# One common offset modulo 512 bytes for all tensor-engine tiles, later scaling and splitting of the key latents, and four gate-weight buffers in an attention layer

## The chip, the core and the metric

The kernel runs on one core of a Trainium2 chip. The metric is device time in microseconds (us): the median of three runs before is 604.2 us (603.97 to 605.96). TensorE is PE in the profile, with PEld for its weight loads; VectorE is DVE, ScalarE is ACT, GpSimd is POOL, SyncE is SP. SP only issues DMAs here.

## The reference

One layer of multi-head latent attention over x (1024 tokens by 1024 channels, fp32), then a final norm. Eight heads; a query/key width of 128 plain and 64 rotary columns; 384 query latents and 256 key/value latents.

```
h = rms_norm(x, g)
proj = h @ w_in                       # c_q 384, c_kv 256, k_pe 64, gate 1024
q = rms_norm(c_q, q_norm) @ w_uq      # per head: 128 plain, 64 rotary
kv = rms_norm(c_kv, kv_norm) @ w_ukv  # per head: 128 key, 128 value
q_pe, k_pe = apply_rope(q_pe), apply_rope(k_pe)
s = q_nope . k_nope + q_pe . k_pe     # times 192 ** -0.5
o = softmax(s) @ v
out = rms_norm(x + (o * silu(gate)) @ w_out, final_norm)
```

## The kernel before

Every product is made in three matmuls. An operand is held as a high and a low part in fp32r (`wh`, `wl`; `xh`, `xl`), and `mm3` (L58 to L61) adds high x high, high x low and low x high into PSUM. Such a pair comes from `split` (L63): POOL writes the high part (L64), DVE subtracts it and writes the low part (L65).

The stages, in program order:

1. L157 to L187: the query latents. Eight steps over the input channels, each with 18 matmuls of 512 columns; xh and xl of the step are made on the way.
2. `rstd_x` (L208) computes the row norms of x; `stream(3)` and `stream(4)` (L245) the key latents `craw[3]`, `craw[4]` with 48 matmuls each. `stream` loads its weights in two halves `gwr` (256 KB each), splits them into `gwh` and `gwl` and multiplies; `gwh` and `gwl` have two buffers each (the pool `gp`, L115), `gwr` has two.
3. `latent_norm` (L233) makes a row of 1/rms for the query latents ("rq") and for the key latents ("rk"). The row goes to DRAM (`rq_d`, `rk_d`) and comes back broadcast to all partitions in `gate[:, 7]`; then DVE scales the latents with it (L243). The scaled query latents are split into cq_h, cq_l (L311, L312), the scaled key latents into kv_h (POOL, L315) and kv_l (DVE, L316).
4. `stream_gate(0)` to `stream_gate(7)` (L261): the output gate, tiles g_6 to g_13, 48 matmuls each. Between them stand four `rope_half` (L340), two head groups g by two halves of the tokens: 18 matmuls into two PSUM tiles `ab`, the rotation on DVE and POOL (L353 to L355), a high copy on ACT (L356), a low part on DVE (L357), and four DMA writes of 256 KB to `qpe_d` in DRAM (L359). t0, t1, hi and lo live in three `rooms` (L338), taken in turn. The weights of a head group are two `load_q` (L366): a load into `wq_r`, which has one buffer (tag `w_r`, shared with the wk and wv loads), and a split.
5. Attention (L434 to L499): 64 score tiles s, each two halves of five matmuls with 512 columns (`q` with `k`, then `qpe` with `kk`), softmax, exchange through DMA, and values: 32 tiles pv of 24 matmuls with 256 columns. k, q and v of a head are made between them.
6. The output projection (L501 to L619): eight token tiles for the first half of the output columns, eight for the second, eight heads of three matmuls each. Its weights `woh`, `wol` of the first half have a pool of their own (but the last head's); those of the second half lie in the places of v, q and, for heads 6 and 7, of `kk_h`, `kk_l` (L519).

A tile scheduler sets the order of the instructions on each engine when the program is built; DMAs of one engine are issued in order. The pools set the addresses in SBUF. In the built program the scratch for DMAs takes the first 16384 bytes of each partition, and the pools follow. The offset of a tile within its partition, modulo 512 bytes, comes out like this (before): xh, xl, gwh, gwl, wpe 288; wh, wl of the first stage 256; cq_h, cq_l, kv and the weights wq, wk 256; q, k, v, qpe, wv and o_split 480; kk 192; pt 352; woh, wol 256 in the first output half, and 480 or 192 (the places of kk) in the second.

Of the kernel before, what the change touches and what calls it, by code (L numbers as in the profile page):

```python
# [8 lines left out]
F32 = mybir.dt.float32  # L9
F32R = mybir.dt.float32r  # L10
AF = mybir.ActivationFunctionType
ALU = mybir.AluOpType
AX = mybir.AxisListType

P = 128
# [5 lines left out]
QR = 384  # L21
KR = 256
EPS = 1e-6
KD = D // P
# [5 lines left out]
def kernel(  # L30
# [21 lines left out]
    nc = tc.nc  # L52
    mm = nc.tensor.matmul

    def f32(ap):
        return ap.bitcast(F32)
# [24 lines left out]
    const = ctx.enter_context(tc.tile_pool(name="const", bufs=1))  # L81
# [3 lines left out]
    ps_t = pctx.enter_context(tc.tile_pool(name="ps_t", bufs=2, space=bass.MemoryType.PSUM))  # L85
    ps_a = pctx.enter_context(tc.tile_pool(name="ps_a", bufs=2, space=bass.MemoryType.PSUM))

    g_sb = const.tile([P, KD + 5], F32, name="g_sb")
    qpe_d = dram.tile([H, 4, 32, L], F32, name="qpe_d")

    row_d = {name: dram.tile([P, KD], F32, name=f"{name}_d") for name in ("rx", "sq", "sk", "rq", "rk")}
    kk_h = const.tile([P, L], F32R, name="kk_h")
    kk_l = const.tile([P, L], F32R, name="kk_l")

    def acc(name):
        return ps_a.tile([P, 512], F32, name=name, tag="acc")
# [4 lines left out]
    def halves(half):  # L101
        return slice(half * HT, (half + 1) * HT)
# [3 lines left out]
    def turned_tile(name):  # L106
        return turned.tile([P, 4, L], F32, name=name, tag="g")

    home = [turned_tile("craw_a"), turned_tile("craw_b")]
    craw = [home[0][:, i] for i in range(4)] + [home[1][:, 0]]  # L110


    xctx = ExitStack()
    xs = xctx.enter_context(tc.tile_pool(name="xs", bufs=1, side="right"))
    gp = xctx.enter_context(tc.tile_pool(name="gp", bufs=2, side="right"))  # L115
    xp = xctx.enter_context(tc.tile_pool(name="xp", bufs=1, side="right"))
    xh = xp.tile([P, KD, L], F32R, name="xh")
    xl = xp.tile([P, KD, L], F32R, name="xl")
# [15 lines left out]
    def rsqrt(v, s, r):  # L134

        nc.scalar.activation(s, v, AF.Sqrt)
        nc.vector.reciprocal(r, s)
        nc.vector.scalar_tensor_tensor(s, r, -0.5, r, op0=ALU.mult, op1=ALU.mult)
        nc.vector.tensor_mul(s, s, v)
        nc.vector.scalar_tensor_tensor(r, s, 1.5, r, op0=ALU.add, op1=ALU.mult)  # L140

    with ExitStack() as wctx:
# [14 lines left out]
        for k in range(KD):  # L157
# [13 lines left out]
            for hs in [halves(0), halves(1)] if k == 0 else [slice(0, L)]:  # L171
# [3 lines left out]
                    op0=ALU.mult, op1=ALU.subtract,  # L175
# [4 lines left out]
            for m, half in units:  # L180
                ms, hs = slice(m * P, (m + 1) * P), halves(half)
# [8 lines left out]
    gate = gpool.tile([P, H, L], F32, name="gate")  # L190
# [3 lines left out]
    kv_h = kvp.tile([P, 2, L], F32R, name="kv_h")  # L194
    kv_l = kvp.tile([P, 2, L], F32R, name="kv_l")
    rx_sb = xs.tile([P, L], F32, name="rx_sb")
    small = xs.tile([P, 6, KD], F32, name="small")
    ssx, mx, rx, v_s, s_s, r_s = (small[:, i] for i in range(6))

    def row_of(name):  # L200
        return row_d[name].rearrange("p j -> (p j)").unsqueeze(0)

    def spread(name, compact, row):

        nc.sync.dma_start(row_d[name], compact)
        nc.sync.dma_start(row, row_of(name).partition_broadcast(P))
# [23 lines left out]
            nc.scalar.copy(line[:, halves(half)], total(cs, half, name)[0:1])  # L230
        nc.sync.dma_start(row_of(name), line)

    def latent_norm(ms, sums, n, name, row):  # L233

        nc.sync.dma_start(v_s, row_d[sums])
        nc.vector.tensor_mul(v_s, v_s, mx)
        nc.vector.tensor_scalar(v_s, v_s, 1.0 / n, EPS, op0=ALU.mult, op1=ALU.add)
        rsqrt(v_s, s_s, r_s)
        nc.vector.tensor_mul(r_s, r_s, rx)
        spread(name, r_s, row)  # L240
        for m in ms:
            c = craw[m]
            nc.vector.scalar_tensor_tensor(c, c, g_sb[:, KD + m:KD + m + 1], row, op0=ALU.mult, op1=ALU.mult)  # L243
# [17 lines left out]
    def stream_gate(i):  # L261
        ps = stream(6 + i)
        gt = gate[:, i]
        nc.vector.tensor_mul(gt, ps, rx_sb)
        nc.scalar.activation(gt, gt, AF.Silu)
# [4 lines left out]
    latent_sums((0, 1, 2), "sq")  # L270
    ps = stream(4)
    nc.scalar.copy(craw[4], ps)
    latent_norm((0, 1, 2), "sq", QR, "rq", gate[:, 7])
    latent_sums((3, 4), "sk")


# [26 lines left out]
        nc.scalar.copy(kk_h[d], kp[0:DR])  # L303
        nc.vector.tensor_sub(kk_l[d], kp[0:DR], f32(kk_h[0:DR]))

    latent_norm((3, 4), "sk", KR, "rk", gate[:, 7])
    cqp = cctx.enter_context(tc.tile_pool(name="cqp", bufs=1))
    cq_h = [cqp.tile([P, L], F32R, name=f"cq_h{m}") for m in range(3)]
    cq_l = [cqp.tile([P, L], F32R, name=f"cq_l{m}") for m in range(3)]
# [1 line left out]
        nc.scalar.copy(cq_h[m], craw[m])  # L311
        nc.vector.tensor_sub(cq_l[m], craw[m], f32(cq_h[m]))  # L312
    stream_gate(0)
    for m in range(2):
        nc.gpsimd.tensor_scalar(kv_h[:, m], craw[3 + m], 1.0, 1.0, op0=ALU.mult, op1=ALU.mult)  # L315
        nc.vector.tensor_sub(kv_l[:, m], craw[3 + m], f32(kv_h[:, m]))  # L316

    def load_split(shape, src, tag, bufs, pool=None):
        pool = pool or wts
        wh = pool.tile(shape, F32R, name=f"{tag}_h", tag=f"{tag}_h", bufs=bufs)  # L320
# [6 lines left out]
    def load_q(src):  # L327
        return load_split([P, 3, P], src, "wq", 2)
# [6 lines left out]

    rope_sb = home[1][:, 1:3]
    nc.sync.dma_start(rope_sb, rope_q.rearrange("c p t -> p c t"))
    rooms = [(home[0][:, 0], home[0][:, 1]), (home[0][:, 2], home[0][:, 3]), (home[1][:, 0], home[1][:, 3])]  # L338

    def rope_half(g, half, w):  # L340

# [18 lines left out]

    for i in range(1, H):
        stream_gate(i)
        if i < 5:
            g, half = (i - 1) // 2, (i - 1) % 2
            if half == 0:
                w_rope = [load_q(wqp[2 * g + j]) for j in range(2)]  # L366
            rope_half(g, half, w_rope)
# [4 lines left out]


    ps_a = ctx.enter_context(tc.tile_pool(name="ps_b", bufs=4, space=bass.MemoryType.PSUM))
    at = ctx.enter_context(tc.tile_pool(name="attn", bufs=2, side="right"))

    def split_tiles(name):
        hi = at.tile([P, 2, HT], F32R, name=f"{name}_h", tag="pt_h", bufs=3)
# [57 lines left out]
    def scores(u, q, kx, qpe):  # L436
        half, qs = (u % 8) // 4, slice((u % 4) * P, (u % 4 + 1) * P)
        s = wide("s")
        qpe_s = qpe[half][:, qs]
        for kb in range(2):  # L440
            ks = halves(kb)
            mm3(s[:, ks], q[half][0][:, qs], q[half][1][:, qs], kx[kb][0], kx[kb][1], True, False)
            mm(s[:, ks], lhsT=qpe_s, rhs=kk_h[:, ks], start=False, stop=False)  # L443
            mm(s[:, ks], lhsT=qpe_s, rhs=kk_l[:, ks], start=False, stop=True)  # L444
        if u % 4 == 0:
            square[u // 4] = turned_tile("probs").rearrange("p j (k t c) -> p j k t c", k=8, t=4)
        p_t = square[u // 4][:, :, :, u % 4]
        nmx = at.tile([P, 1], F32, name="nmx", tag="nmx", bufs=4)
        nc.vector.tensor_reduce(nmx, s, axis=AX.X, op=ALU.max, negate=True)  # L449
        sm = at.tile([P, 1], F32, name="sm", tag="sm", bufs=4)  # L450
        nc.scalar.activation(  # L451
            p_t.rearrange("p j k c -> p k j c"), s.rearrange("p (k j c) -> p k j c", k=8, j=4),
            AF.Exp, bias=nmx, accum_out=sm,
        )
        rc = at.tile([P, 1], F32, name="rc", tag="rc", bufs=4)
        nc.vector.reciprocal(rc, sm)  # L456
        nc.gpsimd.tensor_scalar(p_t, p_t, rc, 1.0, op0=ALU.mult, op1=ALU.mult)  # L457
        nc.vector.transpose(out=p_t, in_=p_t)  # L458
# [63 lines left out]
        (nc.vector if k % 2 else nc.gpsimd).tensor_sub(wl, wr, f32(wh))  # L522
        w_o[nh].append((wh, wl))

    ss = const.tile([P, 2, KD], F32, name="ss")

    def out_start(nh, t, product=True):

        ts = slice(t * P, (t + 1) * P)
# [58 lines left out]

    def out_rstd(t):
        mean_square(t, 1)  # L590
        s, r = (at.tile([P, 1], F32, name=f"y{c}", tag=f"y{c}") for c in "sr")
        rsqrt(ss[:, 0, t:t + 1], s, r)
        return r

# [28 lines left out]
    for u in range(U + 10):  # L623
        h, i = u // 8, u % 8
# [129 lines left out]
```

## Time and profile before

| what | value |
|---|---|
| runs, median of 3 | 604.2 us |
| profiled execution | 605.06 us |
| its span (first to last instruction) | 603.0 us |
| PE busy | 585.5 us, 97% |
| DVE / ACT / POOL busy | 71% / 46% / 36% |

The profiled execution is 0.86 us above the median, and 2.06 us of it lie outside the span. A matmul's busy time in the profile (0.39 us) overlaps the next one's, so the pace of PE is read from the distance between the starts of two matmuls. In rows of the timeline the last bracket gives the idle time ahead of the instruction and what ended it.

### The profile page before, as it was taken

How to read it: one execution, taken by the hardware profiler on the slowest of the kernel's cores; microseconds unless marked ns; L12 is line 12 of the kernel's file. 1: busy time of each engine (PE TensorE's matmuls, PEld its weight loads, DVE VectorE, ACT ScalarE, POOL GpSimd, SP SyncE). 2: the span in 40 equal slices, each digit the busy share in tenths (PEclk: the TensorE clock that was granted, in tenths of full speed). 3: DMA queues.
4: the chain of work that ended last, by engine and by line, in shares of the span. 5: the costliest groups of instructions: out<-in, count | busy, mean ns of one | idle time of the engine just before them, and what ended most of it. 6: DMA issues, size and time to landing. Idle time of an engine off the chain costs nothing.

```text
span 603.0 us, 8667 instructions
## 1 busy us (share of the span) xinstructions
PE 585.5 (97%) x2988; PEld 492.5 (82%) x2988; DVE 429.6 (71%) x632; ACT 277.3 (46%) x435; POOL 218.7 (36%) x195
## 2 busy tenths in 40 slices
PE   9999999898999999999999999999999979999995
PEld 6888878676778888888988889888888868978885
DVE  5613587537414789899878899798987996783663
ACT  4348562102102564556554545454545573653642
POOL 3314502324211344554334354334542663563000
PEclk9999999989999999999999999999999999999999
DMA  8646322242411175566654747356645975431332
GB/s 311 237 119 238 96 72 56 74 129 80 156 48 58 39 170 125 123 149 143 153 128 109 177 107 160 91 128 154 138 101 131 262 180 142 116 103 52 123 139 104
DMA packets 35534, 78.71 MB, mean 131 GB/s; under 512 B 7266, under 2 KB 10850, under 8 KB 35428
## 3 DMA queue, kind: packets, MB, share of 16 engines
q1 hardware_dynamic: 34196, 76.08, 47.0%
q10 hardware_dynamic: 1296, 2.10, 0.9%
q8 instruction: 23, 0.38, 0.3%
q14 instruction: 19, 0.16, 0.1%
HBM read 36.19 MB, written 8.41 MB: 74 GB/s over the span
## 4 chain that ended last, share of the span: by engine, by line
PE 65%; DVE 10%; DMA 10%; issue 6%; SPq 4%; ACT 3%; POOL 2%; ACTq 0%; DVEq 0%; POOLq 0%
PE o L59 4%; PE o L60 4%; PE o L61 4%; PE pv L59 4%; PE pv L60 4%; PE pv L61 4%; PE s L443 4%; PE s L444 4%; PE s L59 4%; PE s L60 4%; PE s L61 4%; SPq L468 3%; PE g L61 3%; PE g L59 3%; PE g L60 3%
## 5 line engine op out<-in xcount | busy, mean ns | idle before, releaser
L457 POOL TENSOR_SCALAR probs<-probs,rc 128x1024 f32<-128x1024 f32 x64 | 82.1, 1285 | 109.5 <-DVE rc L456 88.6
L451 ACT ACTIVATE probs<-s,nmx 128x1024 f32<-128x1024 f32 x64 | 71.4, 1115 | 71.2 <-DVE nmx L449 67.3
L476 ACT CAST pt_h<-d 128x1024 fp32r<-128x1024 f32 x64 | 66.0, 1051 | 45.6 <-PE pv L61 20.1
L458 DVE STREAM_TRANSPOSE probs<-probs 128x1024 f32<-128x1024 f32 x64 | 78.8, 1233 | 6.4 <-POOL probs L457 5.8
L449 DVE TENSOR_REDUCE nmx<-s 128x1 f32<-128x1024 f32 x64 | 76.9, 1207 | 6.8 <-PE s L444 6.6
L59 PE MATMUL pv<-pt_h,v_h 128*128 128x256 f32 x256 | 72.3, 283 | 2.0 <-ACT pt_h L476 2.0
L60 PE MATMUL pv<-pt_l,v_h 128*128 128x256 f32 x256 | 72.1, 282 | 0.9 <-DVE pt_l L478 0.9
L61 PE MATMUL pv<-pt_h,v_l 128*128 128x256 f32 x256 | 71.9, 281 | 0.0
L61 PE MATMUL g<-xh,gwl 128*128 128x512 f32 x160 | 64.2, 401 | 4.6 <-DVE gwl L65 4.6
L59 PE MATMUL g<-xh,gwh 128*128 128x512 f32 x160 | 63.8, 399 | 0.9 <-POOL gwh L64 0.8
L481 POOL TENSOR_TENSOR pt_l<-d,pt_h 128x512 fp32r<-128x512 f32 x32 | 47.9, 1496 | 45.1 <-ACT pt_h L476 25.9
L60 PE MATMUL g<-xl,gwh 128*128 128x512 f32 x160 | 63.3, 396 | 0.0
L59 PEld LDWEIGHTS pv<-pt_h,v_h 128*128 128x128 f32 x256 | 48.2, 188 | 4.4 <-ACT pt_h L476 3.0
L59 PE MATMUL s<-k_h,q_h 128*128 128x512 f32 x128 | 50.4, 396 | 1.2 <-ACT probs L451 1.2
L60 PEld LDWEIGHTS pv<-pt_l,v_h 128*128 128x128 f32 x256 | 48.1, 188 | 3.5 <-DVE pt_l L478 1.1
L443 PE MATMUL s<-kk_h,qpe 128*128 128x512 f32 x128 | 50.7, 396 | 0.0
L444 PE MATMUL s<-kk_l,qpe 128*128 128x512 f32 x128 | 50.7, 396 | 0.0
L60 PE MATMUL s<-k_l,q_h 128*128 128x512 f32 x128 | 50.3, 393 | 0.0
L61 PE MATMUL s<-k_h,q_l 128*128 128x512 f32 x128 | 50.2, 392 | 0.0
L61 PEld LDWEIGHTS pv<-pt_h,v_l 128*128 128x128 f32 x256 | 48.2, 188 | 2.4
L478 DVE TENSOR_TENSOR pt_l<-d,pt_h 128x1024 fp32r<-128x1024 f32 x32 | 42.8, 1337 | 6.5 <-ACT pt_h L476 4.8
L60 PE MATMUL o<-wol,o_split 128*128 128x512 f32 (+1 forms) x118 | 45.1, 382 | 0.0
(194 smaller groups left out, 1288.5 us busy)
## 6 DMA issues: line engine op xcount, KB each, us to landing
d<-probs SPq DMA_DIRECT2D x256, 128.0 KB, 2.4
gwr<-in_wg SPq DMA_DIRECT2D x20, 256.0 KB, 3.0
craw_b<-in_x SPq DMA_DIRECT2D x8, 512.0 KB, 6.6
qpe<-qpe_d SPq DMA_DIRECT2D x16, 256.0 KB, 3.1
wor<-in_wo SPq DMA_DIRECT2D x16, 256.0 KB, 3.2
xr<-in_x SPq DMA_DIRECT2D x16, 256.0 KB, 2.6
xr<-in_xT SPq DMA_DIRECT2D x7, 512.0 KB, 6.5
qpe_d<-craw_a SPq DMA_DIRECT2D x12, 256.0 KB
```

The source lines that it names most:

```text
L59: mm(ps, lhsT=lh, rhs=rh, start=first, stop=False)
L60: mm(ps, lhsT=lh, rhs=rl, start=False, stop=False)
L61: mm(ps, lhsT=ll, rhs=rh, start=False, stop=last)
L443: mm(s[:, ks], lhsT=qpe_s, rhs=kk_h[:, ks], start=False, stop=False)
L444: mm(s[:, ks], lhsT=qpe_s, rhs=kk_l[:, ks], start=False, stop=True)
L449: nc.vector.tensor_reduce(nmx, s, axis=AX.X, op=ALU.max, negate=True)
L451: nc.scalar.activation(p_t.rearrange("p j k c -> p k j c"), s.rearrange("p (k j c) -> p k j c", k=8, j=4), AF.Exp, bias=nmx, accum_out=sm,)
L457: nc.gpsimd.tensor_scalar(p_t, p_t, rc, 1.0, op0=ALU.mult, op1=ALU.mult)
L458: nc.vector.transpose(out=p_t, in_=p_t)
L476: nc.scalar.copy(hi, src)
L478: nc.vector.tensor_sub(lo, src, f32(hi))
L481: nc.gpsimd.tensor_sub(lo[:, 1], src[:, 1], f32(hi[:, 1]))
```

## The change

- The DMA scratch is 1024 bytes in place of 16384, two unused tiles (`pad_a`, `pad_b`) are put into the pool `const`, `ss` moves there, `small` is longer, and the one-column tiles of the softmax and of the last norm move into a pool `columns`. In the built program every tile that a matmul reads then lies at offset 480 modulo 512 bytes.
- `gwh`, `gwl` get four buffers each in place of two.
- `latent_norm` only makes the row; the scaling is a function `latent_scale`. That of the query latents is called after the rotary key is made (L312 after), that of the key latents after stream_gate(3) with its row in `gate[:, 6]`, their split after stream_gate(4).
- The key latents stay in their places for longer, so `rooms` has two entries in place of three.

```diff
-    gp = xctx.enter_context(tc.tile_pool(name="gp", bufs=2, side="right"))
+    gp = xctx.enter_context(tc.tile_pool(name="gp", bufs=4, side="right"))
...
+    const.tile([P, 72], F32, name="pad_a")
...
+    ss = const.tile([P, 2, KD], F32, name="ss")
+    const.tile([P, 112], F32, name="pad_b")
...
-    small = xs.tile([P, 6, KD], F32, name="small")
+    small = xs.tile([P, 16, KD], F32, name="small")
...
-    def latent_norm(ms, sums, n, name, row):
+    def latent_norm(sums, n, name, row):
...
+    def latent_scale(ms, row):
         for m in ms:
             c = craw[m]
             nc.vector.scalar_tensor_tensor(c, c, g_sb[:, KD + m:KD + m + 1], row, op0=ALU.mult, op1=ALU.mult)
...
-    latent_norm((3, 4), "sk", KR, "rk", gate[:, 7])
+    latent_scale((0, 1, 2), gate[:, 7])
+    latent_norm("sk", KR, "rk", gate[:, 6])
...
     stream_gate(0)
-    for m in range(2):
-        nc.gpsimd.tensor_scalar(kv_h[:, m], craw[3 + m], 1.0, 1.0, op0=ALU.mult, op1=ALU.mult)
-        nc.vector.tensor_sub(kv_l[:, m], craw[3 + m], f32(kv_h[:, m]))
...
-    rooms = [(home[0][:, 0], home[0][:, 1]), (home[0][:, 2], home[0][:, 3]), (home[1][:, 0], home[1][:, 3])]
+    rooms = [(home[0][:, 0], home[0][:, 1]), (home[0][:, 2], home[1][:, 3])]
...
     for i in range(1, H):
         stream_gate(i)
+        if i == 3:
+            latent_scale((3, 4), gate[:, 6])
+        if i == 4:
+            for m in range(2):
+                nc.gpsimd.tensor_scalar(kv_h[:, m], craw[3 + m], 1.0, 1.0, op0=ALU.mult, op1=ALU.mult)
+                nc.vector.tensor_sub(kv_l[:, m], craw[3 + m], f32(kv_h[:, m]))
...
+    columns = ctx.enter_context(tc.tile_pool(name="columns", bufs=4, side="right"))
...
-        nmx = at.tile([P, 1], F32, name="nmx", tag="nmx", bufs=4)
+        nmx = column("nmx")
...
-    nc = bacc.Bacc("TRN2", target_bir_lowering=False, num_devices=1)
+    nc = bacc.Bacc("TRN2", target_bir_lowering=False, num_devices=1, dynamic_dma_scratch_size=1024)
```

The scheduler places the instructions anew. Three places show it; a number at the end of a name is the buffer's, and it differs between the two programs for the same tile. Line numbers of the program after are higher by 3 to 13.

SP, before, from the row of the key latents (rk_d) to the second rotary weight of head group 1 (wq_r_999):

```order
L205 DMA rk_d_75<-small_362 128x8
L359 DMA qpe_d_70<-craw_a_81 4x32x512
L206 DMA gate_352<-rk_d_75 128x1024
L359 DMA qpe_d_70<-craw_a_81 4x32x512
L251 DMA gwr_10_0_1039<-in_wg 128x512
L359 DMA qpe_d_70<-craw_a_81 4x32x512 x2
L251 DMA gwr_10_1_1045<-in_wg 128x512
L323 DMA wq_r_999<-in_wqp 128x384
```

And after (there wq_r_998 is that weight):

```order
L209 DMA rk_d_76<-small_365 128x8
L210 DMA gate_355<-rk_d_76 128x1024
L257 DMA gwr_10_1_1044<-in_wg 128x512
L257 DMA gwr_11_0_1139<-in_wg 128x512
L362 DMA qpe_d_71<-craw_a_84 4x32x512
L257 DMA gwr_11_1_1145<-in_wg 128x512
L362 DMA qpe_d_71<-craw_a_84 4x32x512
L362 DMA qpe_d_71<-craw_b_85 4x32x512 x2
L326 DMA wq_r_998<-in_wqp 128x384
```

The row of the key latents now goes out ahead of all qpe_d writes, and gate weights are loaded further ahead; the wq_r load keeps its place behind the four writes of the first rotary half.

DVE, before, around the scaling of the key latents (L243 on gate_352):

```order
L357 TENSOR_TENSOR craw_a_81<-craw_a_81 128x512
L65 TENSOR_TENSOR gwl_9_0_929<-gwr_9_0_930,gwh_9_0_928 128x512
L243 SCALAR_TENSOR_TENSOR craw_a_81<-craw_a_81,g_sb_69,gate_352 128x1024
L243 SCALAR_TENSOR_TENSOR craw_b_82<-craw_b_82,g_sb_69,gate_352 128x1024
L316 TENSOR_TENSOR kv_l_360<-craw_a_81,kv_h_359 128x1024
L316 TENSOR_TENSOR kv_l_360<-craw_b_82,kv_h_359 128x1024
L264 TENSOR_TENSOR gate_352<-g_8_843,rx_sb_361 128x1024
L357 TENSOR_TENSOR craw_a_81<-craw_a_81 128x512
L65 TENSOR_TENSOR gwl_9_1_935<-gwr_9_1_936,gwh_9_1_934 128x512
```

And after (scaling L249, split of the key latents L371, first products of the rotation L356):

```order
L319 TENSOR_TENSOR cq_l0_646<-craw_a_84,cq_h0_643 128x1024
L65 TENSOR_TENSOR gwl_9_1_932<-gwr_9_1_933,gwh_9_1_931 128x512
L319 TENSOR_TENSOR cq_l1_647<-craw_a_84,cq_h1_644 128x1024
L249 SCALAR_TENSOR_TENSOR craw_a_84<-craw_a_84,g_sb_69,gate_355 128x1024
L249 SCALAR_TENSOR_TENSOR craw_b_85<-craw_b_85,g_sb_69,gate_355 128x1024
L319 TENSOR_TENSOR cq_l2_648<-craw_a_84,cq_h2_645 128x1024
L65 TENSOR_TENSOR gwl_10_0_1037<-gwr_10_0_1038,gwh_10_0_1036 128x512
L371 TENSOR_TENSOR kv_l_363<-craw_a_84,kv_h_362 128x1024
L371 TENSOR_TENSOR kv_l_363<-craw_b_85,kv_h_362 128x1024
L356 TENSOR_TENSOR craw_a_84<-ab_794,craw_b_85 128x512 x2
```

gwl_9_1, the low half of a gate weight, stood behind the scaling and the split of the key latents and stands ahead of both now. The scaling stands ahead of the last query split cq_l2, and the split of the key latents ahead of the first rotation.

PE, before, at the first use of the second rotary weight of head group 1 (wq_h_997):

```order
L60 MATMUL ab_1003<-cq_l2_647,wq_h_991 128x512
L61 MATMUL ab_1003<-cq_h2_644,wq_l_992 128x512
L59 MATMUL ab_1013<-cq_h0_642,wq_h_997 128x512
L60 MATMUL ab_1013<-cq_l0_645,wq_h_997 128x512
L61 MATMUL ab_1013<-cq_h0_642,wq_l_998 128x512
```

And after (wq_h_996). Counted from the program's first matmul, from 0, the first matmul on wq_h_996 is number 524. The first rotary half of head group 0 has its first matmul on the split cq_l0 as number 418, its first on cq_l2 as 441 and its last as 444; before, the last run of that half was numbers 382 to 397.

```order
L60 MATMUL ab_1002<-cq_l2_648,wq_h_990 128x512
L61 MATMUL ab_1002<-cq_h2_645,wq_l_991 128x512
L59 MATMUL g_10_1048<-xh_95,gwh_10_0_1036 128x512
L60 MATMUL g_10_1048<-xl_96,gwh_10_0_1036 128x512
L61 MATMUL g_10_1048<-xh_95,gwl_10_0_1037 128x512
L59 MATMUL ab_1012<-cq_h0_643,wq_h_996 128x512
L60 MATMUL ab_1012<-cq_l0_646,wq_h_996 128x512
L59 MATMUL g_10_1048<-xh_95,gwh_10_0_1036 128x512
L61 MATMUL ab_1012<-cq_h0_643,wq_l_997 128x512
```

Three gate matmuls more stand ahead of that use; behind it PE's queue is in order, as before.

## Rows read from the trace of the kernel before

**Rows 1.** The page: the span, and busy time, share and instructions of each engine.

```profile
span 603.0 us, 8667 instructions
PE 585.5 (97%) x2988; PEld 492.5 (82%) x2988; DVE 429.6 (71%) x632; ACT 277.3 (46%) x435; POOL 218.7 (36%) x195
```

**Rows 2.** Busy time by stretch of the span: stretch, length, busy us (instructions) of PE, PEld, DVE, ACT and POOL, granted TensorE clock, share of the DMA engines, GB/s.

```profile
119.90:126.00 6.10, 5.81 (x14) 4.55 (x15) 4.20 (x7) 1.36 (x3) 2.52 (x2) 0.50 0.48 131
300.00:400.00 100.00, 100.00 (x580) 87.73 (x579) 87.44 (x121) 50.52 (x75) 41.39 (x37) 1.00 0.56 130
```

**Rows 3.** PE's timeline in the second output half: start, busy us, engine, line, operation, out<-in. Between the rows stand matmuls of the same tiles only: six on kk from the first row, then six on woh and wol, then twelve.

```profile
561.63 0.40 PE L59 MATMUL o<-kk_h,o_split 128*128 128x512 f32 x1
...
563.03 0.39 PE L59 MATMUL o<-woh,o_split 128*128 128x512 f32 x1
...
564.42 0.39 PE L59 MATMUL o<-woh,o_split 128*128 128x512 f32 x1
...
567.14 0.40 PE L59 MATMUL o<-kk_h,o_split 128*128 128x512 f32 x1
```

**Rows 4.** PE's timeline in the first output half; from the first row to the second 16 matmuls on woh and wol start.

```profile
545.05 0.40 PE L59 MATMUL o<-woh,o_split 128*128 128x512 f32 x1
...
548.77 0.40 PE L60 MATMUL o<-wol,o_split 128*128 128x512 f32 x1
```

**Rows 5.** PE's timeline over one score tile: ten matmuls from the first row to the second.

```profile
302.60 0.39 PE L59 MATMUL s<-k_h,q_h 128*128 128x512 f32 x1
...
304.91 0.28 PE L59 MATMUL pv<-pt_h,v_h 128*128 128x256 f32 x1
```

**Rows 6.** PE's timeline, matmuls of 256 columns: 11 on pt and v from the first row to the second; in the last output tile 15 on woh and wol (in the places of v and q) from the third to the fourth, then six on kk to the fifth.

```profile
307.11 0.28 PE L60 MATMUL pv<-pt_l,v_h 128*128 128x256 f32 x1
...
308.42 0.40 PE L59 MATMUL s<-k_h,q_h 128*128 128x512 f32 x1
...
590.92 0.28 PE L59 MATMUL o<-woh,o_split 128*128 128x256 f32 x1
...
592.72 0.28 PE L59 MATMUL o<-kk_h,o_split 128*128 128x256 f32 x1
...
593.43 0.28 PE L59 MATMUL o<-woh,o_split 128*128 128x256 f32 x1
```

**Rows 7.** PE's timeline at four places in the gate stage, each with the matmul ahead of a pause and the one behind it.

```profile
117.13 0.39 PE L60 MATMUL g<-xl,gwh 128*128 128x512 f32 x1
120.19 0.79 PE L61 MATMUL g<-xh,gwl 128*128 128x512 f32 x1 [2.67 <-DVE gwl L65]
...
137.39 0.39 PE L61 MATMUL g<-xh,gwl 128*128 128x512 f32 x1
138.60 0.50 PE L59 MATMUL g<-xh,gwh 128*128 128x512 f32 x1 [0.81 <-POOL gwh L64]
138.94 0.40 PE L60 MATMUL g<-xl,gwh 128*128 128x512 f32 x1
140.60 0.50 PE L61 MATMUL g<-xh,gwl 128*128 128x512 f32 x1 [1.27 <-DVE gwl L65]
...
161.24 0.39 PE L60 MATMUL g<-xl,gwh 128*128 128x512 f32 x1
162.08 0.50 PE L61 MATMUL g<-xh,gwl 128*128 128x512 f32 x1 [0.45 <-DVE gwl L65]
```

**Rows 8.** The chain of waits that ended last, from the row of the key latents on, and one piece later: start, us, what.

```profile
101.77 1.40 DMA rk_d<-small
103.18 7.58 DMA gate<-rk_d
110.78 1.30 DVE craw_a L243
112.15 2.03 POOL kv_h L315
114.21 2.77 DVE kv_l L316 x2
...
148.36 11.69 DMA gwr<-in_wg
```

**Rows 9.** SP's timeline: start, us, line, DMA issued. The first is the first write of the first rotary half, the others those of the last half.

```profile
102.19 0.62 SPq L359 DMA_DIRECT2D qpe_d<-craw_a  x1
...
144.41 1.66 SPq L359 DMA_DIRECT2D qpe_d<-craw_a  x2
146.16 2.09 SPq L359 DMA_DIRECT2D qpe_d<-craw_b  x2
...
153.61 0.52 SPq L359 DMA_DIRECT2D qpe_d<-craw_a  x1
```

**Rows 10.** PE's timeline: the first matmul of a run of 16 of the first rotary half (number 382), the last of it (397), and the last of the fourth half.

```profile
92.39 0.39 PE L60 MATMUL ab<-cq_l,wq_h 128*128 128x512 f32 x1
...
95.82 0.40 PE L61 MATMUL ab<-cq_h,wq_l 128*128 128x512 f32 x1
...
149.61 0.40 PE L61 MATMUL ab<-cq_h,wq_l 128*128 128x512 f32 x1
```

**Rows 11.** POOL's timeline: the split of a rotary weight, with its wait.

```profile
128.88 0.51 POOL L64 TENSOR_SCALAR wq_h<-wq_r 128x384 fp32r<-128x384 f32 x1 [3.81 <-DMA wq_r<-in_wqp]
```

**Rows 12.** The page, DMA issues: out<-in, engine, count, KB each, us from issue to landing; and the busiest DMA queue: packets, MB, share of 16 engines.

```profile
q1 hardware_dynamic: 34196, 76.08, 47.0%
...
wq_r<-in_wqn SPq DMA_DIRECT2D x8, 192.0 KB, 2.7
```

More of the change, by code (lines that the diff above doesn't have):

```diff
@@ L272 @@
     nc.scalar.copy(craw[4], ps)
-    latent_norm((0, 1, 2), "sq", QR, "rq", gate[:, 7])
+    latent_norm("sq", QR, "rq", gate[:, 7])
     latent_sums((3, 4), "sk")
@@ L374, with column @@
     ps_a = ctx.enter_context(tc.tile_pool(name="ps_b", bufs=4, space=bass.MemoryType.PSUM))
+    columns = ctx.enter_context(tc.tile_pool(name="columns", bufs=4, side="right"))
     at = ctx.enter_context(tc.tile_pool(name="attn", bufs=2, side="right"))
+    def column(name):
+        return columns.tile([P, 1], F32, name=name, tag=name)
     def split_tiles(name):
@@ L447, in scores @@
         p_t = square[u // 4][:, :, :, u % 4]
-        nmx = at.tile([P, 1], F32, name="nmx", tag="nmx", bufs=4)
+        nmx = column("nmx")
         nc.vector.tensor_reduce(nmx, s, axis=AX.X, op=ALU.max, negate=True)
-        sm = at.tile([P, 1], F32, name="sm", tag="sm", bufs=4)
+        sm = column("sm")
         nc.scalar.activation(
@@ L454, in scores @@
         )
-        rc = at.tile([P, 1], F32, name="rc", tag="rc", bufs=4)
+        rc = column("rc")
         nc.vector.reciprocal(rc, sm)
@@ L523, in load_w_out @@
         w_o[nh].append((wh, wl))
-    ss = const.tile([P, 2, KD], F32, name="ss")
     def out_start(nh, t, product=True):
@@ L590, in out_rstd @@
         mean_square(t, 1)
-        s, r = (at.tile([P, 1], F32, name=f"y{c}", tag=f"y{c}") for c in "sr")
+        s, r = (columns.tile([P, 1], F32, name=f"y{c}", tag=f"y{c}", bufs=2) for c in "sr")
         rsqrt(ss[:, 0, t:t + 1], s, r)
```

## The prediction

> **What bounds the kernel now.** I read the page's engine table first: PE is busy 585.5 of 603.0 us [rows 1], so a gain must come from a faster pace of PE or from its pauses. The windows say that inside attention nothing makes PE wait, though DVE is at 87% (the second window of [rows 2]). So I went to PE's timeline and measured distances between starts.
>
> Two paces show. In the second output half the moving operand o_split lies at 480 modulo 512. With weights at 480, twelve matmuls take 2.72 us, 0.2267 each; six on kk (at 192) take 1.40, 0.2333 each; the six right behind them, at 480 again, still 1.39 [rows 3]. Same engine, shape and output tile; only the place of the weights differs. In the first half (weights at 256) 16 take 3.72, 0.2325 each [rows 4]. A score tile mixes six matmuls at equal offsets with four on kk and takes 2.31 for ten [rows 5]. With 256 columns no such step shows: 0.120 at equal offsets (15 in 1.80), 0.118 on kk (6 in 0.71), 0.119 for pv (480 against 352; 11 in 1.31) [rows 6].
>
> [...]
>
> **The change, part by part.**
>
> *Alignment.* At 0.2267 for every 512-column matmul:
> - scores: 2.31 - 2.267 = 0.043 per tile, 64 tiles: 2.8
> - first output half: 8 x 21 = 168 matmuls x 0.0058 = 1.0
> - second output half: per token tile 1.40 + 1.39 - 12 x 0.2267 = 0.07, seven tiles: 0.5
> - first stage (288 against 256): 8 steps x 18 = 144 x at most 0.0058 = 0.8; PE also follows loads there, so half: 0.4
> - 256 columns (768 in pv): 0. By [rows 6] the bounds are 768 x 0.001 = 0.8 either way.
>
> Sum -4.7. Bounds: the offset explains nothing, 0; and all 640 score matmuls gain as [rows 4] do, -6.6.
>
> *Pauses.* Distance less one pace: 3.06 - 0.23 = 2.83, 0.98, 1.43 and 0.61, together 5.85 [rows 7]. The slow stretch costs half of 6.10, 3.05. The first pause is DVE's: gwl_9_1 stands behind the key latents' scaling and split, and those behind the broadcast that lands at 110.78 [rows 8]. In the new order gwl_9_1 stands ahead of both. The others are splits finished too late, because a load of gate weights goes out only when the two buffers are free; the last of them landed 11.69 after its issue, behind four qpe_d writes [rows 8, 9]. With four buffers g_10_1 and both halves of g_11 are issued ahead of those writes. Sum -8.9.
>
> What is late next I looked for in the new order, and found one place.
>
> *A new pause before matmul 524.* It needs wq_h_996. That weight's load has one buffer, so it is issued late, and it stands behind the four qpe_d writes of the first rotary half, while PE's queue behind 524 is in order: gate matmuls whose weights are ready wait too. Step by step:
> - PE gets there at 92.39 + (524 - 382) x 0.227 = 124.6 [rows 10], less the first stage's 0.4: 124.2.
> - The first rotary half now ends with number 444, at 92.39 + 63 x 0.227 - 0.4 = 106.3. From such an end to the first write took 3.8 (149.61 + 0.23 to 153.61) and 6.1 (95.82 + 0.23 to 102.19) [rows 9, 10]: first write at 110.1 to 112.4.
> - A load behind four such writes landed at 160.05, with the first write at 144.41: 15.64 [rows 8, 9]. So the weight lands at 125.7 to 128.0.
> - POOL's split takes 0.51 [rows 11], with hand-overs 0.65: PE goes on at 126.4 to 128.7, a pause of 2.2 to 4.5.
> - DVE now makes the key latents' split (2.03 and 2.77 [rows 8]) ahead of the rotation; part of it comes in here, so up to 2 more. I take 4.0.
>
> After a pause of 2.83 the clock fell to 0.50 for 6.1 us [rows 2]; the pauses of 1.43 and below show no such stretch. One of 4.0 lies beyond the first, so 3.05 mostly applies: 2.4. Together +6.4, bounds 0 (the load as quick as the other wq_r loads, 2.7 [rows 12]) and +9.6 (6.5 and 3.05).
>
> That a load behind the writes is so slow is the trace's own reading: 11.69 against 2.7 for the same kind of issue. [...]
>
> *The last query split.* The key latents' scaling stands ahead of cq_l2, which number 441 needs, at 92.39 + 59 x 0.227 - 0.4 = 105.4. Before, the key row landed at 110.78, and 7.58 of that was the broadcast beside qpe_d writes [rows 8]. The writes now come behind it. If only the broadcast shrinks, to the 2.7 of a load that has no writes ahead [rows 12], the row lands at 105.9, and two scalings of 1.30 and a split taken as long put cq_l2 at 109.8: a pause of 4.4. Were the row as late as before, 9.3. But the row's short DVE chain also comes earlier, since in the new order no rotation stands between its steps; 4.4 us earlier make the pause 0. I add 0.8, close to that end. Bounds 0 and 9.3.
>
> *At nothing.* The kv split is needed only by the first keys, some 60 us later. The smaller scratch: the loads and writes go through hardware queues [rows 12], bounds zero and a few tenths. Two rooms for three: a rotation waits for its writes; only number 578 and later could feel it, price in the new pause's upper bound. The pool `columns` keeps its buffer counts.
>
> Sum: -4.7 - 8.9 + 6.4 + 0.8 = -6.4 against the profiled execution's 605.06: 598.7. That execution is 0.86 above the median, so 597.8.
>
> **The rivals.** All times below are on the median's basis (604.2).
>
> *The load comes in time.* The writes are spread out enough, or the first half ends early, so that 524 doesn't wait. For it: PE's way to 124 is long, and the lower bound of the pause is only 2.2. Against: all four writes stand ahead of the load, and 15.64 is measured. 604.2 - 4.7 - 8.9 = 590.6.
>
> *Offsets don't matter.* The 0.2333 of kk could belong to the place itself, not to its distance from o_split, and the change then does not do what it says. 604.2 - 8.9 + 7.2 = 602.5. Against: two different unequal places, 256 and 192 against 480, give nearly one pace, and 480 against 480 gives 0.2267 once six matmuls behind a switch are over [rows 3, 4]. [...]
>
> *Slower: the key row holds the last query split.* One place, number 441. The order of DVE puts a DMA round trip ahead of work that PE needs within the same ten microseconds. At the upper bound PE stands for 9.3, and the clock's 3.05 follows: 604.2 - 4.7 - 8.9 + 6.4 + 9.3 + 3.05 = 609.4. It decides from a pause of about 4 there on (7.2 less 3.05), a row that lands after 105.7. For it: in the trace that row came last in the chain [rows 8]. Against: what made it late now stands behind it.
>
> **How the numbers follow.** Forecast 0.62 (594.5 to 601, from the new pause's 2.2 with 1.5 of clock to 6 with 3.05, with 0.5 either way for the alignment), load in time 0.13, offsets don't matter 0.13, slower 0.07. The 0.05 left are smaller new waits, 600 to 603. The range takes in the second rival nearly whole and most of what lies between forecast and first: 592 to 602.5. About 0.3%, 1.8 us, is what a measurement here can tell from no change: within 602.4 to 606.0 lies half of the offset rival and a part of the last 0.05, 0.09; above, 0.07 and a little for a milder key-row stall, 0.08; below, 0.83.
>
> **What would show it.** 0.227 between starts in a score tile (2.27 for ten) and all over the output projection; no pause at 117, 138, 140 and 161; one pause of 2 to 6 us near 124 to 128 before an ab matmul, with POOL's wq_h and DMA wq_r as what ended it, and a stretch at 0.50 behind it; no pause at the cq_l2 matmuls. A score tile still at 2.31 proves the first term wrong; a pause of more than 4 near 105 the last; a run through 524 without a stop the third.

## The result and the profile after

The changed kernel takes 599.47 us (median of 4, 597.58 to 600.1) against 604.48 for the kernel before (median of 4): a ratio of 0.9908, 95% interval 0.9879 to 0.9937, 5.0 us less. The forecast was 6.4 less (597.8), with a range of 592 to 602.5. The profiled execution took 599.3.

The page after, span and engines, answering to [rows 1]:

```profile
span 597.3 us, 8664 instructions
PE 579.0 (97%) x2988; PEld 494.0 (83%) x2988; DVE 433.0 (72%) x632; ACT 277.3 (46%) x435; POOL 218.9 (37%) x195
```

The share of PE is the same 97%; 5.7 us are gone from its span. The starts of the first matmul of each stage in PE's timeline divide the span up to its last matmul. The stages are those of the kernel's text; the gate stage runs from the first g to the first q matmul, attention from there to the first o. The last two columns part the difference: the pauses, which are distances between starts more than 0.06 us above 0.227 (0.118 for 256 columns; matmuls at half clock are among them), and the rest, which is the pace.

| stage | before | after | difference | by pauses | by pace |
|---|---|---|---|---|---|
| to the first g | 39.59 | 39.23 | -0.35 | +0.5 | -0.9 |
| gate stage | 146.00 | 142.33 | -3.67 | -3.0 | -0.6 |
| attention | 310.09 | 309.46 | -0.63 | +0.6 | -1.2 |
| output projection | 100.50 | 99.43 | -1.07 | +0.2 | -1.3 |

Two thirds come from the gate stage. The waits of PE, kernel before, then after, both from 60 to 180 us of the span (PE's line, what it waited for, us in total, times, the longest):

```profile
PE g L61 <- DVE gwl L65: 4.6, 4, 2.7
PE g L59 <- POOL gwh L64: 0.8, 1, 0.8
```

```profile
PE ab L59 <- POOL wq_h L64: 4.4, 1, 4.4
```

Five waits for gate weights have become one wait for a rotary weight. PE's timeline after, at that place, and a window of the time behind it (columns as in [rows 2]):

```profile
123.33 0.39 PE L61 MATMUL g<-xh,gwl 128*128 128x512 f32 x1
128.08 0.79 PE L59 MATMUL ab<-cq_h,wq_h 128*128 128x512 f32 x1 [4.37 <-POOL wq_h L64]
```

```profile
128.10:134.50 6.40, 6.40 (x16) 5.06 (x17) 3.25 (x4) 1.06 (x1) 0.51 (x1) 0.53 0.42 148
```

There are 4.75 us between the two starts, so a pause of 4.52; then 16 matmuls in 6.40 us at a clock of 0.53, where 16 x 0.227 = 3.63 would do: 2.8 more. SP's timeline before it, and the pieces of the chain of waits that lead to it:

```profile
111.58 0.62 SPq L362 DMA_DIRECT2D qpe_d<-craw_a  x1
...
113.75 0.54 SPq L362 DMA_DIRECT2D qpe_d<-craw_a  x1
114.35 1.56 SPq L362 DMA_DIRECT2D qpe_d<-craw_b  x2
116.33 2.08 SPq L326 DMA_DIRECT2D wq_r<-in_wqp  x1
```

```profile
115.76 0.54 DVE wq_l L65
...
116.33 11.04 DMA wq_r<-in_wqp
...
127.54 0.50 POOL wq_h L64
```

Read upward: the matmul waits for POOL's split, that for the load, which lands 11.04 after its issue, behind four writes; and the load is issued at 116.33, right when DVE's wq_l of the weight before it, in the same buffer, is done. From the first write to landing it is 127.37 - 111.58 = 15.8.

The paces: one score tile, and 16 matmuls of the first output half, both after (as [rows 5] and [rows 4]):

```profile
305.13 0.40 PE L59 MATMUL s<-k_h,q_h 128*128 128x512 f32 x1
...
306.29 0.39 PE L59 MATMUL s<-k_h,q_h 128*128 128x512 f32 x1
...
307.43 0.28 PE L59 MATMUL pv<-pt_h,v_h 128*128 128x256 f32 x1
...
540.17 0.39 PE L60 MATMUL o<-wol,o_split 128*128 128x512 f32 x1
...
543.80 0.39 PE L61 MATMUL o<-woh,o_split 128*128 128x512 f32 x1
```

The output projection has come down to 3.63 for 16, 0.227 each. The score tile has hardly moved: 2.30 in place of 2.31, its first five matmuls 1.16 and its last five 1.14.

The 0.6 of pace in the gate stage come from somewhere else. There the gate's operands lay at 288 and the query latents and their weights at 256, equal within each product, and still the first matmuls behind a change from one to the other were slow. A run of 18 behind gate matmuls, five matmuls from row to row, before and then after:

```profile
106.97 0.39 PE L59 MATMUL ab<-cq_h,wq_h 128*128 128x512 f32 x1
...
108.13 0.39 PE L61 MATMUL ab<-cq_h,wq_l 128*128 128x512 f32 x1
```

```profile
111.09 0.39 PE L59 MATMUL ab<-cq_h,wq_h 128*128 128x512 f32 x1
...
112.22 0.39 PE L61 MATMUL ab<-cq_h,wq_l 128*128 128x512 f32 x1
```

That is 1.16 against 1.13, where five at 0.227 make 1.13; nearly every such change in the gate stage cost about 0.03 before, and after, at full clock, the runs behind one start at 0.227.

### The profile page after: what moved, and what is told of

Read it like the earlier page. It is cut to its first block, busy times and chain, and to the rows that moved or that the text cites. A ratio compares the mean times of both kernels' runs of the same rounds, so it can differ in the third digit from the quotient of the medians.

```text
span 597.3 us, 8664 instructions
## 1 busy us (share of the span) xinstructions
PE 579.0 (97%) x2988; PEld 494.0 (83%) x2988; DVE 433.0 (72%) x632; ACT 277.3 (46%) x435; POOL 218.9 (37%) x195
## 4 chain that ended last, share of the span: by engine, by line
PE 77%; DVE 8%; DMA 6%; issue 3%; SPq 2%; ACT 2%; POOL 0%; ACTq 0%; DVEq 0%; POOLq 0%
PE s L59 4%; PE s L60 4%; PE s L456 4%; PE pv L59 4%; PE s L457 4%; PE s L61 4%; PE pv L60 4%; PE pv L61 4%; PE o L61 4%; PE o L60 4%; PE g L59 4%; PE g L60 4%; PE o L59 4%; PE g L61 4%; PE q L60 2%
## 5 line engine op out<-in xcount | busy, mean ns | idle before, releaser
L470 POOL TENSOR_SCALAR probs<-probs,rc 128x1024 f32<-128x1024 f32 x64 | 80.9, 1268 | 111.0 <-DVE rc L469 85.3
L494 POOL TENSOR_TENSOR pt_l<-d,pt_h 128x512 fp32r<-128x512 f32 x32 | 46.0, 1438 | 46.1 <-ACT pt_h L489 29.4
L61 PE MATMUL g<-xh,gwl 128*128 128x512 f32 x160 | 62.5, 391 | 0.0
L491 DVE TENSOR_TENSOR pt_l<-d,pt_h 128x1024 fp32r<-128x1024 f32 x32 | 45.1, 1410 | 5.2 <-ACT pt_h L489 4.6
```

Of the source, the lines that this page charges most:

```text
L61: mm(ps, lhsT=ll, rhs=rh, start=False, stop=last)
L491: nc.vector.tensor_sub(lo, src, f32(hi))
L494: nc.gpsimd.tensor_sub(lo[:, 1], src[:, 1], f32(hi[:, 1]))
```

## The experiments

Theory: equal offsets set the pace of 512-column matmuls; the four gate buffers removed the old pauses; the new one is the late load behind the writes. Rivals: the pace follows the place or nothing at all; the later scaling removed the pauses; matmul 524 waits for something else too. The four executions of the changed kernel lie 2.5 us apart, so where an experiment has one run, the reading rests on its trace, and its time can only support it.

### The common offset alone

The kernel before with the memory side of the change and nothing of its order.

```diff
+    const.tile([P, 72], F32, name="pad_a")
...
+    ss = const.tile([P, 2, KD], F32, name="ss")
+    const.tile([P, 112], F32, name="pad_b")
...
-    small = xs.tile([P, 6, KD], F32, name="small")
+    small = xs.tile([P, 16, KD], F32, name="small")
...
+    columns = ctx.enter_context(tc.tile_pool(name="columns", bufs=4, side="right"))
...
-    nc = bacc.Bacc("TRN2", target_bir_lowering=False, num_devices=1)
+    nc = bacc.Bacc("TRN2", target_bir_lowering=False, num_devices=1, dynamic_dma_scratch_size=1024)
```

> The kernel before with the memory side of the change alone: every matmul operand at 480, order of the instructions and buffer counts as before. If equal offsets set the pace: 512-column matmuls at 0.227 in the first stage and the output projection, a score tile at 2.27 to 2.30, the pauses near 117, 137, 139 and 161 still there, time 2.5 to 4.7 us below before. If offsets don't matter: paces as before (0.2325 in the first output half, 2.31 for a score tile) and the time of before within 1 us. If the gain of the change was in its new order alone, this kernel shows none of it.

602.6 us (median of 10) against 604.99: ratio 0.9958 (0.9942 to 0.9974), 2.4 less by the medians and 2.5 by the ratio, whose interval makes 1.6 to 3.5. PE's timeline, a pause in the gate stage and 16 matmuls of the first output half:

```profile
116.77 0.40 PE L60 MATMUL g<-xl,gwh 128*128 128x512 f32 x1
119.84 0.80 PE L61 MATMUL g<-xh,gwl 128*128 128x512 f32 x1 [2.67 <-DVE gwl L65]
...
545.11 0.39 PE L59 MATMUL o<-woh,o_split 128*128 128x512 f32 x1
...
548.73 0.39 PE L60 MATMUL o<-wol,o_split 128*128 128x512 f32 x1
```

The pause of 2.67 is there as in [rows 7], and the pace is 3.62 for 16. So the offset works by itself, at the lower end of what was expected, and leaves the pauses alone.

### Only kk at another offset

```diff
-    const.tile([P, 72], F32, name="pad_a")
...
-    const.tile([P, 112], F32, name="pad_b")
+    const.tile([P, 184], F32, name="pad_b")
```

> The changed kernel, but kk_h and kk_l at 192 modulo 512, all else at 480. If unequal offsets cost: the two kk matmuls of each five in a score tile and the six kk matmuls per token tile of the second output half go back to 0.2325 to 0.234, those behind them need some matmuls to recover, and the time is about 2 us longer than the changed kernel; the first output half and the gate stage stay at 0.227. If kk was slow for a reason of its own, it was slow in the changed kernel too and nothing moves. If offsets don't matter, nothing moves.

601.6 us in one run. PE's timeline in the second output half: six on kk from the first row, six on woh and wol from the second, six from the third.

```profile
558.19 0.40 PE L59 MATMUL o<-kk_h,o_split 128*128 128x512 f32 x1
...
559.59 0.39 PE L59 MATMUL o<-woh,o_split 128*128 128x512 f32 x1
...
560.97 0.39 PE L59 MATMUL o<-woh,o_split 128*128 128x512 f32 x1
...
562.33 0.39 PE L59 MATMUL o<-woh,o_split 128*128 128x512 f32 x1
```

1.40, 1.38 and 1.36: the step of [rows 3] is back where kk is, and only there; attention takes 311.40, 1.9 more than after, 1.6 of it by pace. That kk is slow in its own right is out.

### Every operand at 256

```diff
-    const.tile([P, 72], F32, name="pad_a")
+    const.tile([P, 16], F32, name="pad_a")
...
-    small = xs.tile([P, 16, KD], F32, name="small")
+    small = xs.tile([P, 23, KD], F32, name="small")
...
+    columns.tile([P, 56], F32, name="pad_c", bufs=1)
```

> The changed kernel with every matmul operand at 256 in place of 480. If it is the equality that counts: every pace as in the changed kernel (0.227 in gate stage and output projection) and its time within 1 us. If 480 is a good place by itself and 256 a bad one: the output projection at 0.2325 as with weights at 256 before, and all 512-column matmuls up to 5 ns slower, some 8 us.

598.36 us in one run, and in the first output half:

```profile
540.43 0.39 PE L59 MATMUL o<-woh,o_split 128*128 128x512 f32 x1
...
544.06 0.39 PE L60 MATMUL o<-wol,o_split 128*128 128x512 f32 x1
```

3.63 for 16, with weights at 256, where [rows 4] had 3.72 with weights at 256 and o_split at 480. It is the equality, not the place. That the length that counts is 512 bytes is not shown: the unequal pairs of 512-column matmuls here (256 with 480, 192 with 480, 288 with 256) also differ modulo 64. By what mechanism unequal places cost time no run shows.

### The probability tiles at other offsets

```diff
-        hi = at.tile([P, 2, HT], F32R, name=f"{name}_h", tag="pt_h", bufs=3)
-        lo = at.tile([P, 2, HT], F32R, name=f"{name}_l", tag="pt_l", bufs=3)
-        return hi, lo
+        hi = at.tile([P, L + 128], F32R, name=f"{name}_h", tag="pt_h", bufs=3)
+        lo = at.tile([P, L + 128], F32R, name=f"{name}_l", tag="pt_l", bufs=3)
+        return [t[:, 32:32 + L].rearrange("p (a b) -> p a b", a=2) for t in (hi, lo)]
```

> The changed kernel with only the probability tiles pt moved to 96 modulo 512, so that the 768 value matmuls of 256 columns have unequal offsets. If equality makes 256-column matmuls slower (0.1198 in the changed kernel against 0.1189 before): 0.118 to 0.119 and about 0.8 us less; the score tile behind them unchanged. If what helps at 512 columns helps at 256 too: 0.120 or more, and up to 4 us more. If the value pace is set by something else: 0.1198.

598.32 us in one run; the mean distance in the 768 value matmuls is 0.1198, as after. The score matmuls go from 0.2291 to 0.2298 on average, since in a tile behind value matmuls not five but nine are slow: the sixth to ninth take 0.2285 to 0.2325 in place of 0.2267. The same edit with 96 in place of 32 puts pt at 352, where it was before; it was made on the kernel of the next experiment:

> The changed kernel with two raw-weight buffers and with pt at 352 modulo 512 as in the kernel before, all other operands at 480. If the place of pt set the pace of the value matmuls: 0.1189 as before in place of 0.1198, 0.7 us less than with pt at 480, the score tiles perhaps 0.3 us more. If it is something else (96 did not move it): 0.1198 and 592.3 within 1 us.

592.99 us (median of 4, ratio to before 0.9789, 0.9771 to 0.9806), the value matmuls again at 0.1198, the score matmuls at 0.2299. So none of these places of pt sets the pace of value matmuls. 96 and 352 equal 480 modulo 128, and the score matmuls behind them still feel the difference, so places equal modulo 128 are not equal enough; whether 256 would do is not tested. Why they took 0.1189 before (0.7 us in all 768) stays open.

### A second buffer for the raw weights

```diff
-        wr = wts.tile(shape, F32, name=f"{tag}_r", tag="w_r")
+        wr = wts.tile(shape, F32, name=f"{tag}_r", tag="w_r", bufs=2)
```

> The changed kernel with two buffers for the raw weights (tag w_r), so that the second rotary weight of head group 1 can be loaded ahead of the qpe_d writes. If the pause of 4.5 us before matmul 524 comes from that load's late issue behind the four writes: no pause there, no stretch at half clock behind it, and 6 to 7.5 us below the changed kernel (592 to 593). If PE waits there for something else as well (the rotation's rooms, DVE), the pause only shrinks or moves, and the gain stays under 3 us.

592.29 us (median of 4), ratio 0.9796 (0.977 to 0.9822) to the kernel before: 12.5 below before and 7.2 below the changed kernel. The window from 120 to 175 us, changed kernel, then this one:

```profile
120.00:175.00 55.00, 50.63 (x212) 41.35 (x211) 19.73 (x26) 7.36 (x9) 10.07 (x12) 0.94 0.28 100
```

```profile
120.00:175.00 55.00, 55.00 (x244) 45.53 (x244) 21.69 (x29) 8.48 (x11) 10.82 (x13) 1.00 0.29 103
```

PE is busy all 55 us at full clock, with 244 matmuls in place of 212 (32 x 0.227 = 7.3 us). POOL's splits of the two weights of head group 1 in this kernel:

```profile
113.04 0.87 POOL L64 TENSOR_SCALAR wq_h<-wq_r 128x384 fp32r<-128x384 f32 x1
115.08 0.51 POOL L64 TENSOR_SCALAR wq_h<-wq_r 128x384 fp32r<-128x384 f32 x1 [1.17 <-PE ab L60]
```

The second is made at 115.08 and no longer at 127.5, and does not wait for a load. Nothing else stops PE at matmul 524. The 7.2 are the medians of two sets of executions; by the two ratios to before it is 6.8.

### The writes of the rotary half spread out

```diff
-    qpe_d = dram.tile([H, 4, 32, L], F32, name="qpe_d")
+    qpe_d = dram.tile([4, H, 32, L], F32, name="qpe_d")
...
-                nc.sync.dma_start(qpe_d[g * 4:(g + 1) * 4, c, :, hs], src)
+                nc.sync.dma_start(qpe_d[c, g * 4:(g + 1) * 4, :, hs].rearrange("h p t -> (h p) t"), src)
...
-        nc.sync.dma_start(f32(qpe), qpe_d[h, :, :, halves(half)].rearrange("c p t -> (c p) t"))
+        nc.sync.dma_start(f32(qpe), qpe_d[:, h, :, halves(half)])
```

> The changed kernel with qpe_d laid out as four parts by 256 rows, so that a write of a rotary half has 128 rows of its own as its slowest dimension on the DRAM side in place of 4; one buffer for the raw weights, as in the changed kernel. If the writes are slow because each goes over few DMA engines: the load behind them lands about 3 us after its issue and not 11, and the pause before matmul 524 shrinks to under 1.5 us or goes, with the half clock behind it, some 5 to 7 us less. If the load is late only because its buffer and the writes' data are late: the pause stays at 3 us or more. The reads of qpe then have 4 as their slowest dimension, and may take longer than 3.1 us each; they have some 15 us to spare.

602.87 us in one run. PE waits for nothing between 60 and 174 us, with one raw-weight buffer and the load still issued behind the four writes (at 116.96): the gate stage takes 134.87, the same as with two buffers. POOL's split of that weight:

```profile
120.58 0.95 POOL L64 TENSOR_SCALAR wq_h<-wq_r 128x384 fp32r<-128x384 f32 x1
```

It starts without a wait, 3.6 us after the load's issue, where after the split came 11.2 later (127.54). So the load's 11 us were the doing of the writes as they were laid out. The 5 to 7 us less of the expectation did not come, because attention takes 320.03 in place of 309.46. Its waits here, from 174 to 500 us, and those of the changed kernel from 180 to 500 below:

```profile
PE s L59 <- ACT probs L464: 4.9, 6, 1.5
PE s L61 <- DVE q_l L429: 2.7, 1, 2.7
PE pv L59 <- ACT pt_h L489: 2.0, 3, 1.1
PE pv L60 <- DVE pt_l L491: 0.9, 1, 0.9
```

```profile
PE pv L59 <- ACT pt_h L489: 2.3, 2, 1.2
PE s L59 <- ACT probs L464: 1.9, 2, 1.2
PE pv L60 <- DVE pt_l L491: 0.5, 1, 0.5
```

The waits make 5.8 of the 10.6; most of the rest are matmuls at half clock behind such waits (0.43 apart from 185 to 188, and again from 484 to 488; the longest on kk is busy 0.628, the median 0.389). The side of 4 has moved from the writes to the 16 reads of qpe, and the wq_r loads of attention land after a median of 5.7 us in this kernel against 2.7 [rows 12]. Behind the wait of 2.7 for q_l stands such a load. In both kernels SP issues two reads of qpe and, 1.45 us after the first, the load, here at 175.81 and in the changed kernel at 182.93. POOL's split of it, here and then in the changed kernel:

```profile
183.11 0.51 POOL L64 TENSOR_SCALAR wq_h<-wq_r 128x384 fp32r<-128x384 f32 x1 [8.06 <-DMA wq_r<-in_wqn]
```

```profile
186.10 0.51 POOL L64 TENSOR_SCALAR wq_h<-wq_r 128x384 fp32r<-128x384 f32 x1 [3.93 <-DMA wq_r<-in_wqn]
```

It comes 7.3 and 3.2 after the issue, so there the reads hold the load. That they cause the other waits too is likely and not shown.

### Two gate buffers again

```diff
-    gp = xctx.enter_context(tc.tile_pool(name="gp", bufs=4, side="right"))
+    gp = xctx.enter_context(tc.tile_pool(name="gp", bufs=2, side="right"))
```

> The changed kernel with two buffers for gwh and gwl, as before; later scaling, two rooms and common offset kept. If the four buffers took the pauses away: pauses of 1 to 3 us before g matmuls near 117, 135 and 138 are back, 4 to 6 us in all, and the pause before the ab matmul near 124 shrinks, since PE comes there later. If the later scaling did it: no pause before g matmuls, and only the one near 124.

602.01 us in one run, 2.5 more than the changed kernel and near the 602.6 of the common offset alone. The old pauses are back, 5.2 us of waits in the gate stage, the largest one here:

```profile
117.20 0.39 PE L60 MATMUL g<-xl,gwh 128*128 128x512 f32 x1
119.67 0.50 PE L61 MATMUL g<-xh,gwl 128*128 128x512 f32 x1 [2.07 <-DVE gwl L65]
```

No pause stands before an ab matmul: PE comes there late enough (the run of ab starts at 126.45). So the four buffers took the old pauses away and, with PE earlier at matmul 524, brought the new one.

### Scaling and split where they were

```diff
-    def latent_norm(sums, n, name, row):
+    def latent_norm(ms, sums, n, name, row):
...
-    latent_scale((0, 1, 2), gate[:, 7])
-    latent_norm("sk", KR, "rk", gate[:, 6])
+    latent_norm((3, 4), "sk", KR, "rk", gate[:, 7])
...
-    rooms = [(home[0][:, 0], home[0][:, 1]), (home[0][:, 2], home[1][:, 3])]
+    rooms = [(home[0][:, 0], home[0][:, 1]), (home[0][:, 2], home[0][:, 3]), (home[1][:, 0], home[1][:, 3])]
```

> The changed kernel with scaling and split of the key latents where they stood before, and three rooms; four gate buffers and common offset kept. If the four buffers are enough by themselves: no pause before a g matmul near 117, the pause before the ab matmul near 124 as long as in the changed kernel or up to 1 us longer, time within 1.5 us of the changed kernel. If the later scaling was needed: a pause of about 2.8 us before a gwl near 117 and the half clock behind it, some 4 to 6 us more.

600.37 us in one run, 0.9 above the changed kernel's median. PE has a single wait between 60 and 174 us:

```profile
122.73 0.39 PE L61 MATMUL ab<-cq_h,wq_l 128*128 128x512 f32 x1
127.68 0.80 PE L59 MATMUL ab<-cq_h,wq_h 128*128 128x512 f32 x1 [4.56 <-POOL wq_h L64]
```

No pause near 117. With two raw-weight buffers on top:

> Two buffers for the raw weights, four gate buffers and the common offset, but scaling and split of the key latents and three rooms as in the kernel before. If the later scaling and the two rooms bring nothing by themselves: the time of the changed kernel with two raw-weight buffers (592.3) within 1.5 us, no pause of PE over 1 us between 90 and 180 us. If the later scaling is needed to keep gate weights ahead of the key row: a pause near 117 and 3 to 6 us more.

592.19 us (median of 4), ratio 0.9776 (0.9755 to 0.9797): the 592.29 again, and the gate stage at 134.87 again. The later scaling and the two rooms bring nothing that can be measured once the buffers are there.

### The kernel before with buffers only

```diff
-    gp = xctx.enter_context(tc.tile_pool(name="gp", bufs=2, side="right"))
+    gp = xctx.enter_context(tc.tile_pool(name="gp", bufs=4, side="right"))
...
-        wr = wts.tile(shape, F32, name=f"{tag}_r", tag="w_r")
+        wr = wts.tile(shape, F32, name=f"{tag}_r", tag="w_r", bufs=2)
...
-    nc = bacc.Bacc("TRN2", target_bir_lowering=False, num_devices=1)
+    nc = bacc.Bacc("TRN2", target_bir_lowering=False, num_devices=1, dynamic_dma_scratch_size=1024)
```

> The kernel before with its own offsets, scaling and rooms; only four gate buffers, two raw-weight buffers and the smaller DMA scratch. If the two effects add: no pause over 1 us between 90 and 180 us, paces of the kernel before (0.2325 in the first output half), and a time 2.5 us (what the common offset gave alone) above the 592.2 of the same kernel with the common offset, 594.7. If the offset is worth what the forecast said, 4.7: 596.9. If the offset gave only through the pauses: 592.2.

595.26 us (median of 5), ratio 0.984 (0.9827 to 0.9853); no wait of PE in the gate stage. It is 3.1 above the same kernel with the common offset (3.9 by the two ratios to before), near the 2.4 of the offset alone, so the two effects add within the spread. The 4.7 of the forecast is too much here as well.

The fastest version is the changed kernel, or the one with the old scaling, with two raw-weight buffers: 592.2 to 592.3, below either kernel of the comparison.

## Why the prediction was right, and where it missed

*Pauses removed.* Right in kind: all four of [rows 7] are gone. The sum was 8.9, of which 3.05 is half of the 6.10 at a clock of 0.50 [rows 2]; the gate stage of before holds 10.45 of pauses by the table's bound, which takes in smaller ones that the forecast left out (0.41 at 86.6 among them). The cause was named by halves: the prediction put the first pause down to the place of the key latents' scaling. The old scaling with four buffers shows no pause at 117, so the buffers alone are enough; late scaling with two buffers still shows the wait, 2.07 long where it was 2.67.

*The new pause.* Right in place, cause and chain. Forecast: PE there at 124.2, first write at 110.1 to 112.4, 15.64 to the landing, a pause of 4.0, 2.4 for the clock. Measured: 123.6, 111.58, 15.8, 4.52, and 2.8. The sum was 6.4 and is 7.3. The writes at 144.41 and 146.16 in [rows 9], from which 15.64 is taken, belong to the third rotary half and not to the last; the number is the same, but the third half took 12.2 from its last matmul to its first write, and the prediction's 3.8 and 6.1 leave that out. Two experiments, each touching one of its two conditions (issued late for want of a buffer; slow behind the writes), remove it whole. With the writes laid out wider the load was expected some 3 us after its issue, and the trace agrees: no wait is left, and the split starts 3.6 after the issue. That each write goes over few DMA engines was the author's assumption, and over how many a transfer went no trace here shows; from 122.00 to 127.30 in the changed kernel, while the load had not landed, the mean busy share of the 16 engines was 0.26.

*The last query split.* 0.8 was added; nothing waits there. The key row came earlier than the 105.9 that was worked out for it: DVE's scaling with it starts at 99.07, and cq_l2 is done at 103.52, 1.2 before number 441 starts at 104.74.

*Alignment: the term that was mis-sized.* Forecast 4.7, measured 2.4 by the experiment with the offset alone and 3.1 between the two pause-free kernels. The output projection (1.3 in pace against 1.5) is near. The first stage gained 0.35 against 0.4, but not as it was argued: its pace gained 0.9, and longer pauses took 0.5 back. The gate stage, which stood at nothing, gained 0.6. The scores were put at 2.8, and attention as a whole gained 0.63. The step that failed is "2.31 - 2.267": it takes 0.2267 for all ten matmuls of a tile. Behind a run of 256-column matmuls the first five of 512 columns are slow even at equal offsets, 0.2322 on average before and after; only the five behind them gain, from 0.2322 to 0.2267, and a tile that follows other 512-column matmuls gains from its start. The mean distance of the 640 goes from 0.2322 to 0.2291, which is 2.0. Against that the value matmuls take 0.1198 in place of 0.1189 (0.7 over 768, inside the bound of 0.8 that the prediction gave), those that make v 0.1195 in place of 0.1183 (0.2 over 192), and the pauses of attention are 0.6 longer: PE's waits there are for probs and pt, which ACT and DVE have not finished. Over all stages the pace gained 4.0, and outside the gate stage longer pauses took 1.3 of it back. [Rows 3] had the warning: six matmuls behind a switch still at 0.232. The bound of 6.6 does not follow from its terms: 3.7 for the scores in place of 2.8 makes 5.6.

*The rivals.* That the load comes in time was wrong, though PE's way there was long. That offsets don't matter is ruled out by the kernels with all operands at 256 (3.63 for 16) and with kk alone at 192 (1.40 for six): with equal work, PE loses 6 ns per matmul to the offsets alone, 0.2325 [rows 4] against 0.2263 with the common offset alone (3.62 for 16). The held query split did not come.

The errors have opposite signs: 3.67 gained in the gate stage where -8.9 + 6.4 + 0.8 gave 1.7, and 2.05 in the rest where 4.7 was forecast. So the sum is nearer the mark than its terms, and that closeness is luck.

## What to carry to other kernels

Where PE is the bound, lay all tiles that are streamed and held by 512-column matmuls at one common offset modulo 512 bytes, not only each pair at its own. Here that gave some 6 ns per matmul where they were unequal (0.2325 to 0.227), less where runs alternate with shorter matmuls (0.2322 to 0.2291 in the scores). When more buffers let PE run ahead, look at once for the next load with one buffer and for what is queued ahead of it; here one more buffer was worth 7.2 us, more than the whole change. Look at the layout of what stands ahead of a load as well: behind writes of 4x32x512 it landed after 11.0 us, behind the same data written as 128 rows it was in use after 3.6. Turning the layout around moved the side of 4 to the reads, and attention took 10.6 longer.

## What the runs showed that was not expected

- In runs of 256-column matmuls equal offsets bring no gain: 0.120 equal and 0.118 to 0.119 unequal [rows 6]; moving pt alone to 96 or 352 leaves 0.1198.
- A 512-column run behind a 256-column one pays for five matmuls or so (2.30 for ten at equal offsets), like a run behind unequal offsets (1.39 for six [rows 3]), and like a run behind matmuls whose operands share another offset (1.16 for five at 256 behind 288).
- With the gate stage free of waits, the clock was granted in full from 120 to 175 us; the half clock behind a pause of 4.52 cost 2.8, and behind one of 2.83 about as much: the 14 distances from 120.19 to 126.21 in the kernel before are 2.8 longer than 14 x 0.227.
